# One minus the forget gate as a sigmoid of the negated logit, in a bidirectional gated recurrence

## The chip, the cores and the metric

The kernel runs on one core of one Trainium2 chip. The metric is the device time of one execution in microseconds (us); less is better. Engine names are those of the profile: PE (TensorE, matrix products), DVE (VectorE), ACT (ScalarE), POOL (GpSimd), SP (SyncE, which issues most transfers).

## The reference, cut to what matters

One encoder layer over 256 tokens of width 2048, in float32. Everything starts with a root mean square norm of `x` and one wide product with `w_in`, whose columns are nine groups of 2048. Five of them feed 16 heads of a gated linear recurrence that runs forward and backward; this is the part that the change touches:

```
def _hgrn2_direction(q, v, f_logit, lb, reverse):
    f = lb + (1.0 - lb) * jax.nn.sigmoid(f_logit)
    log_f = jnp.log(f)
    k = 1.0 - f
    ...
# chunks of 64 tokens, per head of 128
b = jnp.cumsum(log_f, axis=-2)
q_rel = q * jnp.exp(b - b_mid)
k_rel = k * jnp.exp(b_mid - b)
scores = q_rel @ k_rel^T, masked;   o = scores @ v + what the earlier chunks carry
```

`lb` is a lower bound per channel, a softmax over two learned rows. `o` of both directions is summed, normed per head and multiplied by `silu(z_a)`. The other four column groups are a gated convolution of width 3. Both branches go through `w_out`, are added to `x`, get a gated per-layer embedding (`p @ w_ple`, `w_ple_gate`) and a last norm.

## The kernel before, in words

PE does nearly all of its work on float32 operands that were split into a high and a low part of a faster matmul format. `Stream` brings blocks of weights by DMA into three buffers `raw`, and `split` (L120 to L122) makes the pair of parts: ACT copies with a cast (L121), DVE subtracts what the cast kept (L122). Five buffers `spl` hold the parts, and `get` runs three blocks ahead of PE. `gemm_in` makes one group of 256 channels from four such blocks of 1024 columns per partition; `evac` then brings its two banks out of PSUM (ACT's copy `r`, L487, then DVE's sum, L488).

The heads are handled in pairs (`i` = 0 to 7 in the helpers), and two pairs make a round of `two_pairs`, for i = 0, 2, 4, 6. In a round PE makes, for each of its two pairs, the forward logits, the backward logits and `q`. Then come the products for `v` and `z` of all four heads (`gemm_vz`). Work on the heads is laid over these products by a counter: `tick` counts PE's steps, `at(n, fn)` puts a function `n` steps later.

For one pair the steps are these, with 128 channels on the partitions and 256 tokens in a row:

- `mix_forgets` multiplies the logits `xf` (two directions, two heads, so 1024 columns) and `qt` by the norms (POOL, `by_norms`, L492). ACT makes the sigmoid of `xf` in place and of `qt` into `sg`; POOL makes `qt * sg`. Then, in four pieces of 256, ACT makes the logarithm of `f` into `lf` (L623) and DVE overwrites `xf` with `1 - f` (L627), as `sigmoid * noml + oml`, where `oml` is 1 - lb and `noml` its negative.
- `mix_pair` makes running sums `pf` and their distances `dd` on DVE, exponentials of them on ACT (L705 and L706, and a small one, `ge`, L703), then `kr` (`dd`) and `qr` (`pf`) as DVE products (L707, L708). POOL makes `kc`, `qc` and `kx` of them (L716, L722).
- `scores` are PE's products `scps` and `cx` (L735, L779); `outputs` are `o` (L797, L798), whose squares ACT sums up into `ss` (L802) and which DVE copies to `ogz` (L803).
- `last_two` of the round before runs inside the next one: `gate_two` makes `zt` times its sigmoid (ACT `sz`, L637, into the one buffer that `sg` uses too; POOL, L638), `finish_two` takes the root of `ss` (ACT, L642), its reciprocal (DVE, L643) and makes eight products `ogz` per round (DVE, L648), and `turn` transposes them on PE (`ogt`, L658).

The framework orders each engine's instructions by priority, except where a block is marked as fixed. Some calls raise the priority of what is needed soon (`high_priority`), the splits above all. Once built, each engine works off its list in order: an instruction that waits holds up all behind it on its engine.

Of the kernel before, what the change touches and what calls it, by code (L numbers as in the profile page):

```python
# [8 lines left out]
F32 = mybir.dt.float32  # L9
F32R = mybir.dt.float32r  # L10
U32 = mybir.dt.uint32
AF = mybir.ActivationFunctionType
ALU = mybir.AluOpType
# [4 lines left out]
P = 128  # L18
D = 2048
T = 256  # L20
# [117 lines left out]
def tile_hymba_encoder(  # L138
# [15 lines left out]
    act, dve, pool, pe = nc.scalar, nc.vector, nc.gpsimd, nc.tensor  # L154
    out2 = out[0].rearrange("(m p) d -> p m d", p=P)

    const = ctx.enter_context(tc.tile_pool(name="const", bufs=1))
# [7 lines left out]
    xp = xctx.enter_context(tc.tile_pool(name="xp", bufs=1, side="left"))  # L165
# [69 lines left out]
    rx, rb, rf, most, dummy = (few[:, 2 * j : 2 * j + 2] for j in range(5))  # L235
# [21 lines left out]
    cvw, th = vec[:, 3:6, :], vec[:, 6:10, :].rearrange("p (d j) c -> p d j c", d=2)  # L257


    wz = const.tile([P, P], F32, name="wz")  # L260
    dve.memset(wz, 0.0)

    act.activation(dummy[:, 0:1], wz[:, 0:1], AF.Copy)
# [6 lines left out]
    ident = const.tile([P, P], F32, name="ident")  # L270
# [1 line left out]
    ones = const.tile([P, 1], F32, name="ones")  # L272
    pool.memset(ones, 1.0)

    early = const.tile([P, 2048], F32, name="early")
    smask = early[:, 0:T]
    pool.memset(smask, 1.0)
    pool.memset(smask.rearrange("p (c t) -> p c t", t=CH)[:, :, 0:1], 0.0)
# [3 lines left out]
    for j in range(4):  # L282
        sgn = 1 if j < 2 else -1
        pool.affine_select(
            out=tri[:, j, :], in_=tri[:, j, :], compare_op=ALU.is_ge, fill=0.0, base=0,
# [9 lines left out]
        dve.memset(t, 0.0)  # L295


    mx = const.tile([P, 2, 16], F32, name="mx")
    et = const.tile([P, 2, 2, 16], F32, name="et")
    esum = const.tile([P, 2, 16], F32, name="esum")  # L300
    lb = const.tile([P, 2, 16], F32, name="lb")
    oml = const.tile([P, 2, 16], F32, name="oml")
    noml = const.tile([P, 2, 16], F32, name="noml")

    def lower_bounds():
        dve.tensor_tensor(out=mx, in0=th[:, :, 0, :], in1=th[:, :, 1, :], op=ALU.max)
        for j in range(2):
            dve.tensor_tensor(out=et[:, :, j, :], in0=th[:, :, j, :], in1=mx, op=ALU.subtract)
        act.activation(et, et, AF.Exp)
        dve.tensor_tensor(out=esum, in0=et[:, :, 0, :], in1=et[:, :, 1, :], op=ALU.add)  # L310
        dve.reciprocal(out=esum, in_=esum)
        dve.tensor_tensor(out=lb, in0=et[:, :, 0, :], in1=esum, op=ALU.mult)
        dve.tensor_scalar(lb, lb, 2.0**-63, None, op0=ALU.max)
        dve.tensor_tensor(out=oml, in0=et[:, :, 1, :], in1=esum, op=ALU.mult)
        dve.tensor_scalar(noml, oml, -1.0, None, op0=ALU.mult)


    pend = []
# [54 lines left out]
    rbc = const.tile([P, T], F32, name="rbc")  # L373
    rbc2 = early[:, T : 2 * T]
    ss8 = const.tile([P, 2, 4], F32, name="ss8")
    rw = [const.tile([P, P], F32, name=f"rw{m}") for m in range(2)]

    def load_tokens(m):
        nc.sync.dma_start(xf32[:, 8 * m : 8 * m + 8].rearrange("p k t -> p (k t)"), xtok[:, m])
# [12 lines left out]
    def x_norms():  # L392
        dve.tensor_reduce(out=rx, in_=ss8, op=ALU.add, axis=AX.X)
        act.activation(rx, rx, AF.Sqrt, bias=epst, scale=1.0 / D)
        dve.reciprocal(out=rx, in_=rx)
        for m in range(2):
            dve.tensor_copy(rw[m], rx[:, m : m + 1].broadcast_to([P, P]))

    def norms_spread():
        rps = psm.tile([P, 512], F32, tag="y", name="rps")  # L400
        for m in range(2):
            pe.matmul(rps[:, m * P : (m + 1) * P], lhsT=rw[m], rhs=ident, start=True, stop=True)
        dve.tensor_copy(rbc, rps[:, :T])  # L403
        dve.tensor_tensor(out=rbc2, in0=rbc, in1=rbc, op=ALU.mult)

# [84 lines left out]
    def by_norms(t, r, n):  # L490

        pool.tensor_tensor(out=t, in0=t, in1=r.unsqueeze(1).broadcast_to([P, n, T]), op=ALU.mult)  # L492
# [27 lines left out]
    ap_ = actx.enter_context(tc.tile_pool(name="ap", bufs=1, side="right"))  # L520
    for m in range(2):
        at(2 + m, lambda m=m: load_tokens(m))
    for c in range(4):
        at(6 + c, lambda c=c: x_squares(c))
    at(11, x_norms)
    at(14, norms_spread)


# [78 lines left out]
    def c64(t):  # L607
        return t.rearrange("p h (c t) -> p h c t", t=CH)

    def mix_forgets(i, xf, qt):  # L610

        by_norms(xf.rearrange("p a b t -> p (a b) t"), rbc, 4)
        by_norms(qt, rbc, 2)
        act.activation(xf, xf, AF.Sigmoid)
        sg = ap_.tile([P, 2, T], F32, tag="sg", name=f"sq{i}")
        act.activation(sg, qt, AF.Sigmoid)
        pool.tensor_tensor(out=qt, in0=qt, in1=sg, op=ALU.mult)

        lf = ap_.tile([P, 2, 2, T], F32, tag="lf", name=f"lf{i}")
        for d in range(2):  # L620
            for h in range(2):
                hd = 2 * i + h
                act.activation(  # L623
                    lf[:, d, h, :], xf[:, d, h, :], AF.Ln,
                    bias=lb[:, d, hd : hd + 1], scale=oml[:, d, hd : hd + 1],
                )
                dve.tensor_scalar(  # L627
                    xf[:, d, h, :], xf[:, d, h, :], noml[:, d, hd : hd + 1], oml[:, d, hd : hd + 1],
                    op0=ALU.mult, op1=ALU.add,
                )  # L630
        return lf

# [34 lines left out]
    def mix_pair(i, xf, qt, lf, here=False):  # L667
# [6 lines left out]
        dv = [dd[:, d] for d in range(2)]  # L674
        lfl = lf.rearrange("p a b c -> p (a b c)")
        for h in range(2):
            place(
                dve.tensor_tensor_scan(
                    out=pv[0][:, h, :], data0=smask, data1=lf[:, 0, h, :], initial=0.0, op0=ALU.mult, op1=ALU.add
# [5 lines left out]
                    out=pv[1][:, h, :], data0=lfl[:, o : o + T], data1=smask, initial=0.0, op0=ALU.add, op1=ALU.mult  # L685
# [4 lines left out]
        for h in range(2):  # L690
            dve.tensor_tensor(
                out=df4[:, h], in0=pf4[:, h], in1=pf4[:, h, :, 31:32].broadcast_to([P, 4, CH]), op=ALU.subtract
            )
            dve.tensor_tensor(
                out=db4[:, h], in0=pb4[:, h, :, 32:33].broadcast_to([P, 4, CH]), in1=pb4[:, h], op=ALU.subtract
# [8 lines left out]
        for d in range(2):  # L704
            act.activation(pv[d], dv[d], AF.Exp)  # L705
            act.activation(dv[d], dv[d], AF.Exp, scale=-1.0)  # L706
            dve.tensor_tensor(out=dv[d], in0=xf[:, d], in1=dv[d], op=ALU.mult)  # L707
            dve.tensor_tensor(out=pv[d], in0=qt, in1=pv[d], op=ALU.mult)  # L708
        qr, kr = pf, dd

# [3 lines left out]
        for dst, src, d, half in ((kc, kr, 0, 0), (qc, qr, 0, 1), (kc, kr, 1, 1), (qc, qr, 1, 0)):  # L714
            g = ge[:, d, :, 1 - half : 5 - half : 3]
            pool.tensor_tensor(  # L716
                out=c64(dst[:, d]), in0=c64(src[:, d, :, half * P : (half + 1) * P]),
                in1=g.unsqueeze(3).broadcast_to([P, 2, 2, CH]), op=ALU.mult,
# [93 lines left out]
    def two_pairs(i):  # L812
# [28 lines left out]
        for e in range(2):  # L841
            xf = ap_.tile([P, 2, 2, T], F32, tag="xf", name=f"xf{i + e}", bufs=2)
            qt = ap_.tile([P, 2, T], F32, tag="qt", name=f"qt{i + e}")
            first3 = i + e == 0

            kick = ({}, {}, {}) if i + e == 0 else (TURNED, {} if i and e else TURNED, TURNED)
            for j, (c, dst) in enumerate(((B_FF, xf[:, 0]), (B_FB, xf[:, 1]), (B_Q, qt))):

                acc, offset = acc3[j] if first3 else gemm_in(c, i + e, kick[j]), 500 if e and j == 2 else 200
                evac(acc, lambda m, dst=dst: dst[:, m, :], ap_, offset)  # L850

            def mix(e=e, xf=xf, qt=qt):
                forgets.append((xf, qt, mix_forgets(i + e, xf, qt)))
                if e == 0:
                    if before:
                        before()
                    steps.append(mix_pair(i, *forgets[0]))

            if first3:

                at(15, mix)
            else:
                mix()
# [5 lines left out]
        if i == 0:  # L869

            at(18, lambda: steps[0][0]())
            at(19, lambda: steps.append(mix_pair(i + 1, *forgets[1])))
            at(46, lambda: out(0))
            at(46, lambda: steps[1][0]())
            at(60, lambda: out(1))
            gemm_two(B_V, i, vt)
            xctx.close()
            xqp = xqctx.enter_context(tc.tile_pool(name="xqp", bufs=1, side="left", reuse_waits="tile"))
            xq.append(xqp.tile([P, len(VZ_SUMS), 4, 2, P], F32R, name="xsum"))
            xq.append(xqp.tile([P, 2, 512], F32, name="xd"))  # L880
            gemm_two(B_ZA, i, zt)
        else:

            at(4, lambda: steps[0][0]())
            gemm_vz(i, vt, zt)
            at(4, lambda: steps.append(mix_pair(i + 1, *forgets[1], here=True)))
            at(12, lambda: out(0))
            at(32, lambda: steps[1][0]())
            at(46, lambda: out(1))
# [34 lines left out]
    for i in range(8):  # L924
# [9 lines left out]
        for m in range(2):  # L934
            ct = 2 * i + m
            dve.tensor_scalar(cg[:, m, :], u[:, m, 0:T], cvw[:, 0, ct : ct + 1], None, op0=ALU.mult)
            for j in (1, 2):
                dve.scalar_tensor_tensor(
                    out=cg[:, m, :], in0=u[:, m, j : j + T], scalar=cvw[:, j, ct : ct + 1],
                    in1=cg[:, m, :], op0=ALU.mult, op1=ALU.add,  # L940
# [13 lines left out]
        for m in range(2):  # L954
            ct = 2 * i + m
            dve.scalar_tensor_tensor(
                out=hb[:, m, :], in0=hb[:, m, :], scalar=cnw[:, ct : ct + 1], in1=sz[:, m, :],
                op0=ALU.mult, op1=ALU.mult,
# [104 lines left out]
    for u in range(2):  # L1063
# [9 lines left out]
        for src, sums, main, other, scale in ((mixa, suma, psg, psm, False), (mixb, sumb, psm, psg, True)):  # L1073
            name = f"p{'ab'[scale]}{u}"
# [10 lines left out]
            for q1, q5, q6, q7 in half([acc[0:2], acc[2:4]], extra, ORDER, SUMS, parts, src, sums, False):  # L1085
                d, v, d7, v7 = tmps
# [179 lines left out]
```

## Time and profile before

| | us |
|---|---|
| median of 3 runs | 1111.57 |
| lowest and highest | 1110.87, 1111.96 |
| the profiled execution | 1112.2 |
| its span, first to last instruction | 1110.5 |

The granted clock of TensorE is 0.998 of the full one in the mean over the span. In the profile, busy time is given by engine; a group of instructions is named by line, engine, operation and tiles (out<-in), with its count, busy time, mean length and the idle time ahead of it with who ended that. A timeline row gives start and length in us from the span's start; "xN" at its end says that N like instructions were merged into it, and what stands in brackets is the idle time of the engine before it.

### The profile page before, as it was taken

Reading aid. Unit: us, or ns where it says so; the run is one execution under the profiler, and the core shown is the slowest. Engines: PE = TensorE matmul, PEld = TensorE weight load, DVE = VectorE, ACT = ScalarE, POOL = GpSimd, SP = SyncE. Lnnn points to the kernel's source line nnn. Section 1 sums busy time; section 2 is a strip of 40 time slices with the busy share of each in tenths; the row PEclk is TensorE's granted clock in tenths of the full one; section 3 lists DMA queues with packets and bytes.
Section 4 is the critical chain, followed back from the end, with each engine's and each line's share of the span. In section 5 each row is a group of like instructions: output and inputs, shape, how many; then the busy total and the mean of one; then the engine's idle time right before and its main releaser. Section 6 shows DMA issues by size and latency. Waiting matters only on the chain.

```text
span 1110.5 us, 16882 instructions
## 1 busy us (share of the span) xinstructions
PE 1100.5 (99%) x6455; PEld 945.7 (85%) x6455; DVE 851.4 (77%) x1127; ACT 677.3 (61%) x946; POOL 269.1 (24%) x215
## 2 busy tenths in 40 slices
PE   9999999999999999999999999999999999999997
PEld 8888888888888888888888888888888888888886
DVE  7799578896889778997657758856667888887673
ACT  6786577667876697575545535535546575575562
POOL 1045015203530325043334223424331000000101
PEclk9999999999999999999999999999999999999999
DMA  9755454564457744758999998999979887887542
GB/s 340 272 187 190 153 190 157 171 242 153 161 162 258 292 152 152 231 172 228 298 310 250 270 334 231 282 345 254 288 196 306 318 299 286 286 312 253 193 133 76
DMA packets 69808, 260.44 MB, mean 235 GB/s; under 512 B 7008, under 2 KB 16608, under 8 KB 52192
## 3 DMA queue, kind: packets, MB, share of 16 engines
q1 hardware_dynamic: 60480, 242.25, 62.1%
q0 software_dynamic: 8960, 16.78, 10.0%
q8 instruction: 51, 0.84, 0.3%
q10 hardware_dynamic: 288, 0.34, 0.1%
q14 instruction: 29, 0.24, 0.1%
HBM read 257.25 MB, written 35.65 MB: 264 GB/s over the span
## 4 chain that ended last, share of the span: by engine, by line
PE 98%; DMA 1%; ACT 0%; SPq 0%; DVE 0%; DVEq 0%; issue 0%; ACTq 0%
PE a L427 37%; PE a L425 19%; PE avz L547 3%; PE avz L548 3%; PE avz L549 3%; PE pg L1027 3%; PE pg L1026 3%; PE pg L1028 3%; PE pa L547 2%; PE pa L548 2%; PE pa L549 2%; PE a L446 1%; PE a L448 1%; PE a L447 1%; PE pb_sc L548 1%; PE pb_sc L549 1%
## 5 line engine op out<-in xcount | busy, mean ns | idle before, releaser
L122 DVE TENSOR_TENSOR spl<-raw,spl 128x1024 fp32r<-128x1024 f32 (+2 forms) x419 | 505.0, 1219 | 163.6 <-ACT spl L121 160.2
L427 PE MATMUL a<-xs,spl 128*128 128x512 f32 x1792 | 617.3, 395 | 0.6 <-ACT spl L121 0.6
L121 ACT CAST spl<-raw 128x1024 fp32r<-128x1024 f32 (+2 forms) x419 | 414.1, 999 | 255.0 <-PE a L425 81.9
L425 PE MATMUL a<-xs,spl 128*128 128x256 f32 x1792 | 483.8, 278 | 0.0
L427 PEld LDWEIGHTS a<-xs,spl 128*128 128x128 f32 x1792 | 332.2, 188 | 73.6 <-ACT spl L121 1.0
L425 PEld LDWEIGHTS a<-xs,spl 128*128 128x128 f32 x1792 | 334.6, 188 | 5.8 <-DVE spl L122 0.5
L1143 POOL TENSOR_TENSOR hh<-hh,fw 128x512 f32<-128x512 f32 (+1 forms) x9 | 11.0, 1227 | 250.7 <-ACT gt L1142 248.0
L487 ACT COPY r<-a 128x256 f32<-128x256 f32 x112 | 40.5, 368 | 37.3 <-PE a L425 35.8
L547 PE MATMUL avz<-spl,xs 128*128 128x512 f32 x138 | 54.0, 391 | 0.0
L549 PE MATMUL avz<-spl,xs 128*128 128x512 f32 x138 | 53.7, 389 | 0.0
L548 PE MATMUL avz<-spl,xs 128*128 128x512 f32 x138 | 53.7, 389 | 0.0
L1026 PE MATMUL pg<-spl,ht 128*128 128x512 f32 (+1 forms) x120 | 45.2, 377 | 0.0
L1027 PE MATMUL pg<-spl,ht 128*128 128x512 f32 (+1 forms) x120 | 45.1, 376 | 0.0
L1028 PE MATMUL pg<-spl,ht 128*128 128x512 f32 (+1 forms) x120 | 45.0, 375 | 0.0
L716 POOL TENSOR_TENSOR qc<-pf,ge 128x256 f32<-128x256 f32 x16 | 18.3, 1148 | 105.8 <-ACT dd L706 91.8
L492 POOL TENSOR_TENSOR xf<-xf,rbc 128x1024 f32<-128x1024 f32 x8 | 19.9, 2486 | 94.0 <-DVE rbc L403 50.2
L121 ACT CAST spl<-early 128x1024 fp32r<-128x1024 f32 (+1 forms) x29 | 28.7, 990 | 19.1 <-PE pb_y L549 7.5
L122 DVE TENSOR_TENSOR spl<-early,spl 128x1024 fp32r<-128x1024 f32 (+1 forms) x29 | 32.9, 1147 | 9.2 <-ACT spl L121 8.8
L547 PE MATMUL pa<-spl,mixa 128*128 128x512 f32 x88 | 34.5, 392 | 0.0
L549 PE MATMUL pa<-spl,mixa 128*128 128x512 f32 x88 | 34.3, 389 | 0.0
L548 PE MATMUL pa<-spl,mixa 128*128 128x512 f32 x88 | 34.2, 389 | 0.0
L716 POOL TENSOR_TENSOR kc<-dd,ge 128x256 f32<-128x256 f32 x16 | 27.7, 1728 | 19.8 <-DVE dd L707 13.6
(321 smaller groups left out, 1641.7 us busy)
## 6 DMA issues: line engine op xcount, KB each, us to landing
raw<-in_w_in_dram SPq DMA_DIRECT2D x106, 1024.0 KB, 6.9
raw<-in_w_in_dram SPq DMA_DIRECT2D x100, 256.0 KB, 3.9
raw<-in_w_out_dram SPq DMA_DIRECT2D x36, 512.0 KB, 5.2
sums<-in_w_out_dram SPq DMA_DIRECT2D x32, 512.0 KB, 10.6
raw<-in_w_in_dram SPq DMA_DIRECT2D x26, 512.0 KB, 5.2
raw<-sums SPq DMA_DIRECT2D x13, 1024.0 KB, 5.3
raw<-in_w_gate_dram SPq DMA_DIRECT2D x9, 1024.0 KB, 5.1
sums<-in_w_out_dram POOLq DMA_DIRECT2D x16, 512.0 KB, 10.1
```

Source lines behind the costliest of these rows:

```text
L121: self.nc.scalar.copy(out=v[:, :, 0], in_=r)
L122: self.nc.vector.tensor_tensor(out=v[:, :, 1], in0=r, in1=v[:, :, 0], op=ALU.subtract)
L425: pe.matmul(a[:, :T], lhsT=lhsT, rhs=xs[:, kt, 0, :], start=False, stop=(kt == NKT - 1))
L427: pe.matmul(a, lhsT=lhsT, rhs=xs[:, kt, :, :].rearrange("p s n -> p (s n)"), start=(kt == 0), stop=False)
L487: act.copy(out=r, in_=acc[m][:, 1, :])
L547: pe.matmul(acc, lhsT=ah, rhs=w[:, 0], start=start, stop=False)
L548: pe.matmul(acc, lhsT=ah, rhs=w[:, 1], start=False, stop=False)
L549: pe.matmul(acc, lhsT=al, rhs=w[:, 0], start=False, stop=stop)
L716: pool.tensor_tensor(out=c64(dst[:, d]), in0=c64(src[:, d, :, half * P : (half + 1) * P]), in1=g.unsqueeze(3).broadcast_to([P, 2, 2, CH]), ...
L1026: pe.matmul(acc[m], lhsT=lh, rhs=wh, start=(kt == 0), stop=False)
L1027: pe.matmul(acc[m], lhsT=lh, rhs=wl, start=False, stop=False)
L1028: pe.matmul(acc[m], lhsT=ll, rhs=wh, start=False, stop=(kt == nk - 1))
```

## The change

`1 - f` is (1 - lb) times (1 - sigmoid), and that is (1 - lb) times the sigmoid of the negated logit. So:

- `mix_forgets` makes the sigmoid of the logits into `lf` and a second one, with scale -1, in place in `xf`. The logarithm then works in place on `lf`. The four DVE operations that made `1 - f` are gone, and so is `noml`.
- In `mix_pair` the product that makes `kr` takes the factor in: four scalar_tensor_tensor of 128x256 (`xf * oml * dd`) stand for two tensor_tensor of 128x512.
- The zeros of PE's warm-up lie in the part of `early` that later holds the first score mask; three small tiles of `lower_bounds` go to another pool, and the spread norms `rw` use a buffer of the tile `s`.

```
-    wz = const.tile([P, P], F32, name="wz")
+    early = const.tile([P, 2048], F32, name="early")
+    wz = early[:, 1024 : 1024 + P]
     dve.memset(wz, 0.0)
...
-    mx = const.tile([P, 2, 16], F32, name="mx")
-    et = const.tile([P, 2, 2, 16], F32, name="et")
-    esum = const.tile([P, 2, 16], F32, name="esum")
+    mx = xp.tile([P, 2, 16], F32, name="mx")
+    et = xp.tile([P, 2, 2, 16], F32, name="et")
+    esum = xp.tile([P, 2, 16], F32, name="esum")
...
-    noml = const.tile([P, 2, 16], F32, name="noml")
...
-        dve.tensor_scalar(noml, oml, -1.0, None, op0=ALU.mult)
...
-    rw = [const.tile([P, P], F32, name=f"rw{m}") for m in range(2)]
...
+        rw.append(ap_.tile([P, 2, P], F32, tag="s", name="rw"))
...
-        act.activation(xf, xf, AF.Sigmoid)
+        lf = ap_.tile([P, 2, 2, T], F32, tag="lf", name=f"lf{i}")
+        act.activation(lf, xf, AF.Sigmoid)
         sg = ap_.tile([P, 2, T], F32, tag="sg", name=f"sq{i}")
         act.activation(sg, qt, AF.Sigmoid)
+        act.activation(xf, xf, AF.Sigmoid, scale=-1.0)
         pool.tensor_tensor(out=qt, in0=qt, in1=sg, op=ALU.mult)
 
-        lf = ap_.tile([P, 2, 2, T], F32, tag="lf", name=f"lf{i}")
         for d in range(2):
             for h in range(2):
                 hd = 2 * i + h
                 act.activation(
-                    lf[:, d, h, :], xf[:, d, h, :], AF.Ln,
+                    lf[:, d, h, :], lf[:, d, h, :], AF.Ln,
                     bias=lb[:, d, hd : hd + 1], scale=oml[:, d, hd : hd + 1],
                 )
-                dve.tensor_scalar(
-                    xf[:, d, h, :], xf[:, d, h, :], noml[:, d, hd : hd + 1], oml[:, d, hd : hd + 1],
-                    op0=ALU.mult, op1=ALU.add,
-                )
...
             act.activation(dv[d], dv[d], AF.Exp, scale=-1.0)
-            dve.tensor_tensor(out=dv[d], in0=xf[:, d], in1=dv[d], op=ALU.mult)
+            for h in range(2):
+                dve.scalar_tensor_tensor(
+                    out=dv[d][:, h], in0=xf[:, d, h], scalar=oml[:, d, 2 * i + h : 2 * i + h + 1], in1=dv[d][:, h],
+                    op0=ALU.mult, op1=ALU.mult,
+                )
             dve.tensor_tensor(out=pv[d], in0=qt, in1=pv[d], op=ALU.mult)
```

With other instructions the framework's order comes out otherwise. PE's order is the same but for names. The lists of ACT, DVE and POOL differ in the rounds; the place below is in the round i = 4, and it repeats at i = 6. There PE makes the logits of pair 5, while ACT, DVE and POOL work on pair 4 and finish pairs 2 and 3 (`zt`, `ss`, `ogz`). A number behind a name is the buffer's.

DVE before, from the reciprocal of `ss` to behind the last product `ogz`:

```order
L643 RECIPROCAL ss_1332<-ss_1332 128x8
L122 TENSOR_TENSOR spl_2830<-raw_2809,spl_2830 128x4x256
L708 TENSOR_TENSOR pf_2755<-qt_2354,pf_2755 128x512
L122 TENSOR_TENSOR spl_2851<-raw_2849,spl_2851 128x4x256
L648 SCALAR_TENSOR_TENSOR ogz_2447<-ogz_2447,ss_1332,zt_1331 128x128 x2
L648 SCALAR_TENSOR_TENSOR ogz_2704<-ogz_2704,ss_1332,zt_1331 128x128 x2
L122 TENSOR_TENSOR spl_2878<-raw_2849,spl_2878 128x4x256
L648 SCALAR_TENSOR_TENSOR ogz_2447<-ogz_2447,ss_1332,zt_1331 128x128 x2
L122 TENSOR_TENSOR spl_2899<-raw_2897,spl_2899 128x4x256
L488 TENSOR_TENSOR xf_2786<-a_5_0_2788,r 128x256
L488 TENSOR_TENSOR xf_2786<-a_5_1_2789,r 128x256
L648 SCALAR_TENSOR_TENSOR ogz_2704<-ogz_2704,ss_1332,zt_1331 128x128 x2
```

DVE in the changed kernel, from the second product with `qt` to behind the last `ogz`:

```order
L709 TENSOR_TENSOR pf_2744<-qt_2344,pf_2744 128x512
L705 SCALAR_TENSOR_TENSOR dd_2745<-xf_2343,oml,dd_2745 128x256 x2
L122 TENSOR_TENSOR spl_2869<-raw_2840,spl_2869 128x4x256
L122 TENSOR_TENSOR spl_2890<-raw_2888,spl_2890 128x4x256
L488 TENSOR_TENSOR xf_2777<-a_5_0_2779,r 128x256
L488 TENSOR_TENSOR xf_2777<-a_5_1_2780,r 128x256
L640 RECIPROCAL ss_1326<-ss_1326 128x8
L645 SCALAR_TENSOR_TENSOR ogz_2439<-ogz_2439,ss_1326,zt_1325 128x128 x3
L122 TENSOR_TENSOR spl_2919<-raw_2888,spl_2919 128x4x256
L645 SCALAR_TENSOR_TENSOR ogz_2439<-ogz_2439,ss_1326,zt_1325 128x128
L122 TENSOR_TENSOR spl_2940<-raw_2938,spl_2940 128x4x256
L645 SCALAR_TENSOR_TENSOR ogz_2696<-ogz_2696,ss_1326,zt_1325 128x128 x4
```

The reciprocal has moved behind the two sums into `xf`, and all eight `ogz` behind it; two more splits stand between them.

ACT before, from the first exponential of pair 4 to the first `sz`:

```order
L705 ACT_TABLE_LOAD
L705 ACTIVATE pf_2755<-dd_2756 128x512
L642 ACT_TABLE_LOAD
L642 ACTIVATE ss_1332<-ss_1332,epst 128x8
L121 CAST spl_2830<-raw_2809 128x4x256
L616 ACT_TABLE_LOAD
L616 ACTIVATE sq_2737<-qt_2354 128x512
L121 CAST spl_2851<-raw_2849 128x4x256
L637 ACTIVATE sz_0_2749<-zt_1331 128x512
```

ACT in the changed kernel, from the first `sz` to the root:

```order
L634 ACTIVATE sz_0_2738<-zt_1325 128x512
L703 ACT_TABLE_LOAD
L703 ACTIVATE dd_2745<-dd_2745 128x512
L121 CAST spl_2869<-raw_2840 128x4x256
L634 ACT_TABLE_LOAD
L634 ACTIVATE sz_1_2741<-zt_1325 128x512
L121 CAST spl_2890<-raw_2888 128x4x256
L487 COPY r<-a_5_0_2779 128x256
L487 COPY r<-a_5_1_2780 128x256
L639 ACT_TABLE_LOAD
L639 ACTIVATE ss_1326<-ss_1326,epst 128x8
```

The root of `ss` stood ahead of the first `sz` and now stands behind both and the two copies `r`; the exponentials of pair 4 have moved ahead of it.

POOL before, from the second multiplication of `qt`:

```order
L617 TENSOR_TENSOR qt_2354<-qt_2354,sq_2737 128x512
L638 TENSOR_TENSOR zt_1331<-zt_1331,sz_0_2749 128x512
L716 TENSOR_TENSOR qc_2779<-pf_2755,ge_2765 128x256
L638 TENSOR_TENSOR zt_1331<-zt_1331,sz_1_2752 128x512
L716 TENSOR_TENSOR kc_2778<-dd_2756,ge_2765 128x256
L716 TENSOR_TENSOR qc_2779<-pf_2755,ge_2765 128x256
```

POOL in the changed kernel, from the same place:

```order
L619 TENSOR_TENSOR qt_2344<-qt_2344,sq_2730 128x512
L717 TENSOR_TENSOR qc_2770<-pf_2744,ge_2754 128x256
L635 TENSOR_TENSOR zt_1325<-zt_1325,sz_0_2738 128x512
L717 TENSOR_TENSOR qc_2770<-pf_2744,ge_2754 128x256
L717 TENSOR_TENSOR kc_2769<-dd_2745,ge_2754 128x256
L723 TENSOR_TENSOR kx_2775<-kc_2769,ge_2754 128x512
L635 TENSOR_TENSOR zt_1325<-zt_1325,sz_1_2741 128x512
```

The second `zt` now has `qc`, `kc` and `kx` between it and the first.

More of the change, by code (lines that the diff above doesn't have):

```diff
@@ L273, in tile_hymba_encoder @@
     pool.memset(ones, 1.0)
-    early = const.tile([P, 2048], F32, name="early")
     smask = early[:, 0:T]
@@ L395, in x_norms @@
         dve.reciprocal(out=rx, in_=rx)
+        rw.append(ap_.tile([P, 2, P], F32, tag="s", name="rw"))
         for m in range(2):
-            dve.tensor_copy(rw[m], rx[:, m : m + 1].broadcast_to([P, P]))
+            dve.tensor_copy(rw[0][:, m], rx[:, m : m + 1].broadcast_to([P, P]))
+    rw = []
     def norms_spread():
@@ L401, in norms_spread @@
         for m in range(2):
-            pe.matmul(rps[:, m * P : (m + 1) * P], lhsT=rw[m], rhs=ident, start=True, stop=True)
+            pe.matmul(rps[:, m * P : (m + 1) * P], lhsT=rw[0][:, m], rhs=ident, start=True, stop=True)
         dve.tensor_copy(rbc, rps[:, :T])
```

## The prediction

> **What bounds the kernel now.** First the page's busy times and its chain, then TensorE's own waits.
>
> ```profile
> PE 1100.5 (99%) x6455; PEld 945.7 (85%) x6455; DVE 851.4 (77%) x1127; ACT 677.3 (61%) x946; POOL 269.1 (24%) x215
> PE 98%; DMA 1%; ACT 0%; SPq 0%; DVE 0%; DVEq 0%; issue 0%; ACTq 0%
> PE wps L266 <- DVE wz L261: 1.1, 1, 1.1
> PE a L427 <- ACT spl L121: 0.6, 1, 0.6
> ```
>
> The last two lines are all the waits of TensorE (PE): 1.7 us, both at the start. From there to its last matmul it always has the next operand. So an operation taken from another engine gains nothing by itself, and the question is only whether some operand of PE comes late in the new order. Gains are bounded by that 1.7 us.
>
> The reserve of the weight stream is in the idle time of ScalarE (ACT), from the page's groups, and by shape:
>
> ```profile
> L121 ACT CAST spl<-raw 128x1024 fp32r<-128x1024 f32 (+2 forms) x419 | 414.1, 999 | 255.0 <-PE a L425 81.9
> L614 ACT ACTIVATE xf<-xf 128x1024 f32<-128x1024 f32 x8 | 8.5, 1062 | 6.9 <-POOL xf L492 6.9
> L627 DVE TENSOR_SCALAR xf<-xf,noml,oml 128x256 f32<-128x256 f32 x32 | 14.8, 472 | 4.6 <-ACT lf L623 4.6
> L707 DVE TENSOR_TENSOR dd<-xf,dd 128x512 f32<-128x512 f32 x16 | 13.6, 851 | 0.6 <-ACT dd L706 0.6
> L938 DVE SCALAR_TENSOR_TENSOR cg<-ub,vec,cg 128x256 f32<-128x256 f32 x32 | 14.5, 477 | 0.2
> ```
>
> The casts that feed PE stood idle 255.0 us, 81.9 of it because PE had not yet freed a buffer: they run ahead of PE.
>
> **The change part by part, by sums.** ACT gains eight 128x1024 sigmoids: 8 x 1.06 = 8.5 us. The new order has 48 table loads for 52, 4 x 1.28 = 5.1 us less, so ACT nets +3.4 us. VectorE (DVE) loses 32 tensor_scalars (14.8 us) and 16 products (13.6), and gets 32 fused products of 128x256, which before shows at L938: 32 x 0.477 = 15.3. DVE nets -13.1 us. All of this lies beside PE and is worth 0, covered by the idle time above; without that cover ACT's sigmoids would cost up to 8.5.
>
> The small edits: the warm-up's zeros are still DVE's first memset; POOL's memset of the score masks now waits for the warm-up matmuls, but POOL has nothing due for 50 us, as this row shows:
>
> ```profile
> 54.29 2.40 POOL L492 TENSOR_TENSOR xf<-xf,rbc 128x1024 f32<-128x1024 f32 x1 [50.18 <-DVE rbc L403]
> ```
>
> `noml`, `mx`, `et`, `esum` and `rw` are 0 too, between +0.2 and -0.2 us (an estimate, one small DVE operation either way).
>
> **The place where the order matters.** The scheduler placed things anew. PE's stream is the same, so what counts is each operand's date against PE's. In the pairs i = 4 and i = 6, the transposes of the gated heads (`ogt`, L658) now depend on work that was pushed back. Before, timeline rows of PE, then DVE, then ACT (start, length):
>
> ```profile
> 300.01 0.39 PE L427 MATMUL a<-xs,spl 128*128 128x512 f32 x1
> 300.36 1.03 PE L658 MATMUL ogt<-ident,ogz 128*128 128x128 f32 x8
> 301.15 0.48 PE L427 MATMUL a<-xs,spl 128*128 128x512 f32 x1
> 417.78 1.03 PE L658 MATMUL ogt<-ident,ogz 128*128 128x128 f32 x8
> 284.04 0.19 DVE L643 RECIPROCAL ss<-ss 128x8 f32<-128x8 f32 x1
> 290.84 1.48 DVE L648 SCALAR_TENSOR_TENSOR ogz<-ogz,ss,zt 128x128 f32<-128x128 f32 x4 [1.20 <-POOL zt L638]
> 292.25 1.21 DVE L122 TENSOR_TENSOR spl<-raw,spl 128x1024 fp32r<-128x1024 f32 x1
> 297.00 0.61 DVE L648 SCALAR_TENSOR_TENSOR ogz<-ogz,ss,zt 128x128 f32<-128x128 f32 x2
> 414.43 0.61 DVE L648 SCALAR_TENSOR_TENSOR ogz<-ogz,ss,zt 128x128 f32<-128x128 f32 x2
> 276.94 0.28 ACT L802 ACTIVATE jk<-o 128x128 f32<-128x128 f32 x1 [0.90 <-PE o L798]
> 279.88 1.28 ACT L705 ACT_TABLE_LOAD   x1
> 281.28 0.64 ACT L705 ACTIVATE pf<-dd 128x512 f32<-128x512 f32 x1
> 281.94 1.28 ACT L642 ACT_TABLE_LOAD   x1
> 283.23 0.30 ACT L642 ACTIVATE ss<-ss,epst 128x8 f32<-128x8 f32 x1
> 293.71 0.64 ACT L487 COPY r<-a 128x256 f32<-128x256 f32 x2
> ```
>
> Eight `ogz` products end at 297.61, PE wants the first four at 300.36 and the others after four transposes of 0.1 us, at 300.76: a reserve of 3 us. At i = 6 it is 415.04 against 417.78.
>
> In the new order ACT's square root `ss` stands behind both COPYs of `r`. The added sigmoid ahead (its start-to-start cost is about 0.97 us) is swallowed by the 0.90 idle at 276.94, so the table load of 279.88 stays within 0.1. From there to the end of the COPYs, 294.35 before, ACT loses one table load and `ss` (1.28 + 0.2) and gains three 128x512 exponentials that came later before (3 x 0.52): 294.4. Then a table load 1.28, the root 0.30, the reciprocal 0.2: 296.2. Behind it on DVE stand 3 `ogz` (0.9), a split (1.13), 1 `ogz` (0.3), a split (1.13), 4 `ogz` (1.1), together 4.5: 300.7. That would just meet 300.76. This is the low end: no loss.
>
> But the same stretch has the GpSimd (POOL) products that these `ogz` need, and they and DVE hold each other up:
>
> ```profile
> 286.49 1.29 POOL L617 TENSOR_TENSOR qt<-qt,sq 128x512 f32<-128x512 f32 x1 [2.40 <-ACT sq L616]
> 288.53 2.28 POOL L638 TENSOR_TENSOR zt<-zt,sz 128x512 f32<-128x512 f32 x1 [0.74 <-ACT sz L637]
> 290.77 0.62 POOL L716 TENSOR_TENSOR qc<-pf,ge 128x256 f32<-128x256 f32 x1
> 292.94 1.68 POOL L638 TENSOR_TENSOR zt<-zt,sz 128x512 f32<-128x512 f32 x1 [1.56 <-ACT sz L637]
> 298.28 5.01 POOL L716 TENSOR_TENSOR kc<-dd,ge 128x256 f32<-128x256 f32 x1 [3.66 <-DVE dd L707]
> 305.51 1.05 POOL L722 TENSOR_TENSOR kx<-kc,ge 128x512 f32<-128x512 f32 x1
> 288.43 1.22 DVE L122 TENSOR_TENSOR spl<-raw,spl 128x1024 fp32r<-128x1024 f32 x1
> 298.12 1.22 DVE L122 TENSOR_TENSOR spl<-raw,spl 128x1024 fp32r<-128x1024 f32 x1
> 299.26 0.68 DVE L708 TENSOR_TENSOR pf<-qt,pf 128x512 f32<-128x512 f32 x1
> 299.86 1.22 DVE L122 TENSOR_TENSOR spl<-raw,spl 128x1024 fp32r<-128x1024 f32 x1
> 301.60 1.22 DVE L122 TENSOR_TENSOR spl<-raw,spl 128x1024 fp32r<-128x1024 f32 x1
> 302.73 0.42 DVE L488 TENSOR_TENSOR xf<-a,r 128x256 f32<-128x256 f32 x1
> ```
>
> Starts on DVE are 1.14 apart behind a split and 0.60 behind `pf` (298.12, 299.26, 299.86). POOL's `kc`, of the shape for which `qc` took 0.62, took 5.01 while DVE went through split, `pf`, split, `dd` and split, and ended 0.57 after DVE turned to an operation that reads PSUM (302.73). Likewise the first `zt` took 2.28 and the second 1.68, each under a split (288.43 to 289.65, and the one of 292.25 that ended at 293.46) and each ending 1.16 to 1.17 after it. So DVE products from SBUF and POOL products run one after the other.
>
> Before, only `qc` stood between the two `zt`. Now `qc`, `kc` and `kx` do, and DVE's `pf` and fused `dd`, which came behind the `ogz` before, fall into the same window. It opens when POOL's `qt` ends, 287.8. From there to the end of the second `zt`, POOL has qc 0.6, zt 1.16, qc 0.6, kc 0.6, kx 1.05, zt 1.16 = 5.2; DVE has pf 0.6, split 1.13, pf 0.6, two fused dd 0.8, two splits 2.26 = 5.4. One after the other: 287.8 + 10.6 = 298.4. The `ogz` that read `zt` queue behind, and the splits behind them: 298.4 + 4.5 = 302.9, which is 2.1 us past 300.76. Nothing else on PE can go first, since its queue is in order. I take this value, because the rows show the two engines excluding each other in just this stretch. Two such places: +4.2 us.
>
> The Trainium skill, SBUF — State Buffer, section "Who interferes with whom", says that a DVE instruction with two SBUF inputs contends with a GpSimd instruction that reads SBUF, and that whichever issues first keeps the pair for that whole instruction. By that, `kc` should have waited for one split; here it waited through four DVE instructions, so waiting can cost more than the page says. By its rule alone, turn and turn about, the sum is the same 4.2.
>
> Two other dates move little. At i = 2 the order has the root where it was. Pair 7 is the nearest:
>
> ```profile
> 495.94 1.92 POOL L722 TENSOR_TENSOR kx<-kc,ge 128x512 f32<-128x512 f32 x1
> 499.07 1.16 PE L779 MATMUL cx<-qc,kx 128*128 128x128 f32 x8
> ```
>
> `kx` is ready 1.2 us early; two fused products for one (2 x 0.477 for 0.851, +0.1) at two steps ahead of it, and POOL's waits for them, eat part of that: I take 0, at most 0.6. The split made at 292.25 is the operand of the last quarter of the product that ends at 300.36. A pair of matmuls takes 0.35 (300.01 to 300.36) and a split serves eight, 2.8 us: it is used from 297.6, four us later. The splits' delay of 2 to 3 us stays inside that: 0.
>
> **The sum.** The profiled execution took 1112.2 us (span 1110.5), 0.6 over the median 1111.57. 1112.2 + 2 x 2.1 = 1116.4 there, so 1115.8 against the median.
>
> **The rivals.**
> 1. No change: DVE and POOL fit into each other's gaps, and `ogz` ends by 300.8 as the plain sum of ACT and DVE says. It decides by one number: if the eighth `ogz` ends before the fifth transpose is due, the loss is 0. For it: DVE waits for ACT in this stretch, so POOL finds gaps. Against: the 5.01 above. Time 1111.6; up to 1.1 us a place still counts here (2.2 in all). Chance 0.30.
> 2. POOL starves for several DVE instructions on end, as `kc` did. DVE's first forced pause is then behind the split that follows the fused products: 287.8 + 0.6 + 1.14 + 0.6 + 0.8 + 1.14, and about 0.6 for an exponential of ACT that `dd` waits for, is 292.7. Only there do qc (0.6) and the first `zt` (1.16) run, to 294.5. The second `sz` of ACT shares its one buffer with the first, so it waits for that `zt`: sz 0.6, cast 1.0, COPYs 0.6, table 1.28, root 0.3 end at 298.3. With the reciprocal and the rest of the second `zt`, 299.1; plus 4.5 is 303.6, or 2.9 a place: 1117.4. Chance 0.18.
> 3. The sigmoid makes the casts late everywhere: 8 x 0.97 = 7.8, 1119.4. Against it the 81.9 us of ACT waiting for PE. Chance 0.03.
> 4. Faster, since DVE has 13 us less: only the 0.6 at the start could shrink. Chance 0.02.
>
> The main case, 1.1 to 2.6 a place, has 0.47.
>
> **How the numbers follow.** A measurement of this kernel tells from no change about 0.2%, 2.2 us. Slower: 0.47 + 0.18 + 0.03 = 0.68; within: 0.30; faster: 0.02. Range: down to 1111.2 (all of rival 1 but its lowest tail), up to 1118.2 (rival 2 plus 0.6 at pair 7). The likeliest case alone gives 1113.8 to 1116.8.
>
> **What would show it.** PE waits of about 2 us at the transposes, put down to DVE `ogz`, near 300 and near 420, and nowhere else; the reciprocal of `ss` at 296 to 298; `zt` behind `kx`. Right in mechanism but wrong in size if the waits are there and short. Wrong altogether if PE shows no waits beyond 1.7 us, or shows them on casts.

## The result, and the profile after

| | before | changed |
|---|---|---|
| median, us | 1111.65 | 1117.55 |
| lowest and highest | 1110.87, 1112.02 | 1116.63, 1120.32 |
| runs | 6 | 6 |
| the profiled execution | 1112.2 | 1117.67 |
| its span | 1110.5 | 1116.0 |

The ratio is 1.0057, 95% interval 1.0045 to 1.0070: the change makes the kernel 0.6% slower. (Here and below a ratio is taken over all runs on one chip; it is not the quotient of the two medians.) The forecast was 1115.8 us with a range of 1111.2 to 1118.2. Sign and range hold, but most of the loss is not where the prediction put it.

First the page of the changed kernel: the busy times, and the chain by engine.

```profile
PE 1105.7 (99%) x6455; PEld 946.0 (85%) x6455; DVE 842.8 (76%) x1110; ACT 678.5 (61%) x950; POOL 261.9 (23%) x215
PE 90%; ACT 3%; DVE 2%; POOL 2%; issue 1%; DMA 1%; DVEq 0%; SPq 0%; POOLq 0%; ACTq 0%
```

DVE lost 8.6 us of work (851.4 before) and ACT gained 1.2 (677.3). The number that matters is PE's: the same 6455 matmuls kept it busy 1105.7 us instead of 1100.5. A wait would show as idle time; here PE is *busy* 5.2 us longer. So the list of PE's waits cannot hold the answer, though the waits that were forecast are in it:

```profile
PE wps L267 <- DVE early L262: 1.1, 1, 1.1
PE ogt L655 <- DVE ogz L645: 0.4, 2, 0.2
```

PE's timeline at the two places, start and length, in the changed kernel:

```profile
299.63 0.80 PE L655 MATMUL ogt<-ident,ogz 128*128 128x128 f32 x5
300.63 0.59 PE L655 MATMUL ogt<-ident,ogz 128*128 128x128 f32 x3 [0.20 <-DVE ogz L645]
300.99 0.47 PE L427 MATMUL a<-xs,spl 128*128 128x512 f32 x1
...
417.66 0.80 PE L655 MATMUL ogt<-ident,ogz 128*128 128x128 f32 x5
418.66 0.59 PE L655 MATMUL ogt<-ident,ogz 128*128 128x128 f32 x3 [0.20 <-DVE ogz L645]
419.02 0.47 PE L427 MATMUL a<-xs,spl 128*128 128x512 f32 x1
```

From the first transpose to the next product PE took 1.36 us at each place (299.63 to 300.99, 417.66 to 419.02), where before took 0.79 (300.36 to 301.15, and 417.78 to 418.57). That is 0.57 us a place, 1.1 in all. The 0.20 in brackets is less than that: the fifth transpose starts at 300.10 and its record lasts 0.33, so the bracket counts only from 300.43 to 300.63, while in the kernel before one transpose starts 0.11 behind the other. The sixth transpose starts 0.06 after the seventh `ogz` has ended (300.57), and that is the piece it reads: `finish_two` makes the four pieces of a pair token half by token half, `turn` reads them head by head.

The rest is found by pairing PE's matmuls by their number in the stream, since both kernels run the same ones in the same order. The 5,244th and the 6,003rd are these, before and then after:

```profile
840.75 0.39 PE L549 MATMUL pa<-spl,mixa 128*128 128x512 f32 x1
1010.03 0.39 PE L1028 MATMUL pg<-spl,ht 128*128 128x512 f32 x1
```

```profile
841.29 0.40 PE L549 MATMUL pa<-spl,mixa 128*128 128x512 f32 x1
1015.08 0.40 PE L1029 MATMUL pg<-spl,ht 128*128 128x512 f32 x1
```

The changed kernel is 0.54 us behind at the first and 5.05 at the second: 4.5 us are lost over 759 matmuls, practically all of it in the 715 of them that belong to the output projection (`half`, moving operand `spl`, stationary operand `mixa`, `mixb`, `suma` or `sumb`). The change does not touch an instruction there. Two windows of that stage, with PE's busy time, count of matmuls, granted clock, DMA share and GB/s, before and then after:

```profile
840.00:920.00 80.00, 80.00 (x355) 1.00 0.92 313
920.00:1000.00 80.00, 80.00 (x363) 1.00 0.82 289
```

```profile
840.00:920.00 80.00, 79.93 (x344) 1.00 0.89 301
920.00:1000.00 80.00, 80.00 (x355) 1.00 0.81 282
```

PE is full in all four and the clock is 1.00 in all four, but 699 matmuls fit where 718 did. In the groups by line and shape, cut to this stage (count, busy us, mean ns of one), before and then after:

```profile
L547 PE MATMUL pb_sc<-spl,mixb 128*128 128x512 f32 x48 | 18.7, 389 | 0.0
L548 PE MATMUL pb_sc<-spl,mixb 128*128 128x512 f32 x48 | 18.7, 389 | 0.0
L549 PE MATMUL pb_sc<-spl,mixb 128*128 128x512 f32 x48 | 18.7, 389 | 0.0
```

```profile
L548 PE MATMUL pb_sc<-spl,mixb 128*128 128x512 f32 x48 | 19.0, 396 | 0.0
L547 PE MATMUL pb_sc<-spl,mixb 128*128 128x512 f32 x48 | 18.9, 394 | 0.0
L549 PE MATMUL pb_sc<-spl,mixb 128*128 128x512 f32 x48 | 18.9, 393 | 0.0
```

Every group of the stage went from 389 to 391 ns before to between 392 and 399, without a wait. 4.5 us over 715 is 6.3 ns a matmul, about what the means show. The record of a matmul overlaps the next one: from start to start the matmuls of this stage are 227 ns apart in the mean before and 233 after, and the expectations below go by this distance.

What did change for these matmuls is where their operands lie. `noml` (128 bytes on each partition) is gone, and `wz`, `mx`, `et`, `esum` and `rw` (2048 bytes together) went into other tiles. All large tiles that are laid out from the left of SBUF (`raw`, `spl`, `xs`, `hh`, `ht`, `sumb`) start 2176 bytes lower; `mixa`, `mixb` and `suma`, laid out from the right, stay. In the built kernels `spl` begins at byte 54208 before and 52032 after, `mixb` at 147392 in both: modulo 1024 that is 960 and 960 before, 832 and 960 after; modulo 256 it is 192 and 192, then 64 and 192.

### The profile page after: what moved, and what is told of

It is laid out like the page before. It is cut to its first block, busy times and chain, and to the rows that moved or that the text cites. A ratio compares the mean times of both kernels' runs of the same rounds, so it can differ in the third digit from the quotient of the medians.

```text
span 1116.0 us, 16883 instructions
## 1 busy us (share of the span) xinstructions
PE 1105.7 (99%) x6455; PEld 946.0 (85%) x6455; DVE 842.8 (76%) x1110; ACT 678.5 (61%) x950; POOL 261.9 (23%) x215
## 4 chain that ended last, share of the span: by engine, by line
PE 90%; ACT 3%; DVE 2%; POOL 2%; issue 1%; DMA 1%; DVEq 0%; SPq 0%; POOLq 0%; ACTq 0%
PE a L427 33%; PE a L425 17%; PE avz L547 3%; PE avz L549 3%; PE avz L548 3%; PE pg L1027 3%; PE pg L1029 3%; PE pg L1028 3%; PE pa L548 1%; PE pa L549 1%; PE pa L547 1%; PE a L448 1%; PE a L446 1%; PE a L447 1%; PE pb_sc L548 1%; PE pb_sc L547 1%
## 5 line engine op out<-in xcount | busy, mean ns | idle before, releaser
L122 DVE TENSOR_TENSOR spl<-raw,spl 128x1024 fp32r<-128x1024 f32 (+2 forms) x419 | 497.6, 1203 | 181.6 <-ACT spl L121 179.9
L944 POOL TENSOR_TENSOR cg<-cg,hb 128x512 f32<-128x512 f32 x8 | 14.6, 1822 | 78.0 <-DVE hb L488 78.0
```

Source lines behind the costliest of these rows:

```text
L122: self.nc.vector.tensor_tensor(out=v[:, :, 1], in0=r, in1=v[:, :, 0], op=ALU.subtract)
```

## The experiments

Two theories. **Placement**: a matmul is slower when its moving and its stationary operand do not agree in their byte offset. **Order**: all of the loss comes from the new order of ACT, DVE and POOL. An unused tile among the constants moves the left side without moving work. The first four ran on one chip, on which the kernel before took 1112.64 us (median of 23), the next four on another (1113.00, median of 23), the last two on a third.

### The shift alone, in the kernel before

```
     oml = const.tile([P, 2, 16], F32, name="oml")
+    gap = const.tile([P, 32], F32, name="gap")
+    pool.memset(gap, 0.0)
     noml = const.tile([P, 2, 16], F32, name="noml")
```

> The kernel before, with one unused 128-byte tile (and one memset of it on GpSimd) among the constants: `raw`, `spl`, `xs`, `hh`, `ht` and `sumb` lie 128 bytes higher, `mixa`, `mixb` and `suma` stay, and no other instruction differs. Placement theory (the output projection's matmuls take longer when `spl` and the `mix` tiles do not lie at the same offset): 1116 us, 1115 to 1117, with the 512-wide matmuls after 840 us about 232 to 236 ns apart where the kernel before has 227, and no wait at `ogt`. Order theory (all of the change's loss comes from the new order of ACT, DVE and POOL): 1111.6 us, like before, 227 ns throughout.

Measured: 1118.22 us, ratio 1.0041 (1.0026 to 1.0056). PE's waits and the same three groups:

```profile
PE wps L266 <- DVE wz L261: 1.1, 1, 1.1
PE a L429 <- ACT spl L121: 0.3, 1, 0.3
```

```profile
L549 PE MATMUL pb_sc<-spl,mixb 128*128 128x512 f32 x48 | 19.0, 395 | 0.0
L550 PE MATMUL pb_sc<-spl,mixb 128*128 128x512 f32 x48 | 18.9, 395 | 0.0
L551 PE MATMUL pb_sc<-spl,mixb 128*128 128x512 f32 x48 | 18.9, 394 | 0.0
```

No wait at `ogt`, the old math and the old order, and yet 394 to 395 ns and most of the loss. The order theory falls for this part: 128 bytes of nothing cost 0.4%. The median lies above the 1115 to 1117 expected, and not only because this chip's kernel before is 1 us slower. In the profiled execution, the fastest of the six at 1115.51, the output projection took 3.9 us longer than in the kernel before; where the slower runs lost more is not shown.

### The shift undone, in the changed kernel

The same two lines behind `oml` in the changed kernel, so that the left side stands 2048 instead of 2176 bytes lower (960 of 1024 again).

> The changed kernel with one unused 128-byte tile (and a memset) among the constants, so that `spl` and the tiles beside it lie 2048 instead of 2176 bytes lower than before. Placement theory: the 512-wide matmuls after 840 us go back to 227 ns; what is left is the two waits at `ogt`, about 0.5 us each: 1112.7 us, 1112.2 to 1113.2. Order theory: 1117.5 us, as the changed kernel.

Measured: 1114.54 us, ratio 1.0018 (1.0007 to 1.0028).

```profile
L549 PE MATMUL pb_sc<-spl,mixb 128*128 128x512 f32 x48 | 18.7, 389 | 0.0
L550 PE MATMUL pb_sc<-spl,mixb 128*128 128x512 f32 x48 | 18.7, 389 | 0.0
L551 PE MATMUL pb_sc<-spl,mixb 128*128 128x512 f32 x48 | 18.7, 389 | 0.0
```

The stage is back at 389 ns. The 1112.7 expected were reckoned from a kernel before at 1111.6; on this chip that was 1112.64, so what is left is 1.9 us, where two waits of 0.5 to 0.6 were expected.

### The sigmoid and the product alone, without and with a tile in `noml`'s place

The two lines of math and the dropped `noml`, with the five small tiles where before has them (left side 128 bytes lower); then the same with the 128 bytes of `gap` put back (nothing moved).

> The sigmoid of the negated logit, the product with `oml` and the dropped tile `noml` alone; `wz`, `mx`, `et`, `esum` and `rw` stay where before has them. `spl` lies 128 bytes lower than before, by the dropped `noml`. Placement theory: 1117.3 us, 1116.5 to 1118, 229 to 241 ns between the 512-wide matmuls after 840 us. If instead the moved small tiles were what costs: 1112.7 us. Order theory: 1117.5 us.

> As the run with the sigmoid and the product alone, with an unused 128-byte tile where `noml` was, so that every large tile lies where it lies in the kernel before. Placement theory: 1112.7 us, 1112.2 to 1113.2, 227 ns after 840 us, two waits at `ogt` of about 0.5 us. Order theory: 1117.5 us.

Measured: 1117.82 us, ratio 1.0050 (1.0031 to 1.0069), without the tile, and 1114.52 us, 1.0012 (1.0003 to 1.0022), with it. One group of the first and of the second:

```profile
L545 PE MATMUL pb_sc<-spl,mixb 128*128 128x512 f32 x48 | 19.0, 395 | 0.0
```

```profile
L547 PE MATMUL pb_sc<-spl,mixb 128*128 128x512 f32 x48 | 18.7, 389 | 0.0
```

The two kernels with the tile (1114.52 and 1114.54) differ by all the moved small tiles, and do not differ in time. So no cost of the moves can be told at intervals of 1 us to either side, the math and its order cost 1 to 2 us, and the 128 bytes of `noml` the rest. The 1112.7 expected with the tile was missed here as in the run before. Set against the kernel before matmul by matmul, both profiled executions lost 1.2 us at the two places of `ogt`; what else they lost lies at different places, 1.9 us between 674 and 752 in this one, 1.3 near 757 and 767 (behind waits for split weights) and 1.1 in the output projection (with another such wait) in the other.

### The other operand moved instead

```
-    mixa = mixp.tile([P, NH * 2 * T + 8], F32R, name="mixa")[:, : NH * 2 * T]
+    mixa = mixp.tile([P, NH * 2 * T + 40], F32R, name="mixa")[:, : NH * 2 * T]
```

> The changed kernel with the pad behind `mixa` at 40 instead of 8 floats: `mixa`, `mixb` and `suma` lie 128 bytes lower and stand again at the offset of `spl` (832 of 1024, for both), which itself stays where the changed kernel has it. If the relative offset of the matmul's two operands decides: 389 ns mean of one in the output projection and the time of the run with the 128-byte tile (about 1114 us on this chip). If it is the place of `spl` alone: 394 to 398 ns and 1117.5 us, as the changed kernel. Order theory: 1117.5 us too.

Measured: 1114.96 us, ratio 1.0015 (1.0004 to 1.0025), with `spl` where the changed kernel has it.

```profile
L547 PE MATMUL pb_sc<-spl,mixb 128*128 128x512 f32 x48 | 18.7, 389 | 0.0
```

So it is the one operand against the other that counts, not where either lies by itself. In the kernel before it is the pad of 8 floats behind `mixa` that puts both at 192 modulo 256; what it is worth was not tried.

### The transposes one step later

```
-                    at(32, lambda e=e: turn(i + e, ogs[e], "yx"[e]))
+                    at(33, lambda e=e: turn(i + e, ogs[e], "yx"[e]))
```

This on top of the changed kernel with the 128-byte tile.

> The changed kernel with the 128-byte tile, and the transposes `ogt` queued one step of the schedule later (33 instead of 32), so that `ogz` is long written when PE comes to them. If the two waits at `ogt` are all that is left of the change's loss: no wait at `ogt`, 0.8 to 1.2 us under the run with the tile alone, and within 0.1% of the kernel before. If the late `ogz` only shows a delay that PE meets elsewhere: the time of the run with the tile alone, with a wait of the same size at another place.

Measured: 1112.99 us, ratio 0.9999 (0.9988 to 1.0009).

```profile
PE wps L267 <- DVE early L262: 1.1, 1, 1.1
PE pa L550 <- DVE spl L122: 0.6, 1, 0.6
```

The wait at `ogt` is gone and with it the rest of the loss: 1.97 us under the run with the moved `mixa`, which shared its chip and has the same order but for this step. That is more than the 1.14 which the two places show. Matmul by matmul, the two profiled executions end 2.35 us apart: 1.1 comes at the two places and 1.5 between 674 and 752, where the run with the moved `mixa` is in the slower rhythm described last below and this one is not (0.3 the other way comes in the output projection). Whether the medians differ for the same reason is not shown. Both causes removed, the kernel stands level with the one before. It isn't faster: PE was full before, and DVE's 8.6 us had nobody waiting for them.

### Which offsets cost

The unused tile at 640, 1152, 384 and 192 bytes, so that `spl` stands 512, 1024, 256 and 64 bytes above the place at which it agrees with the `mix` tiles; one execution each.

> The changed kernel with an unused tile of 640 bytes: `spl` lies 512 bytes above the place at which it agrees with the `mix` tiles modulo 1024. If the offset counts modulo 512 or less: 389 ns mean in the output projection. If it counts modulo 1024 or more: 394 ns or above. Order theory: no difference to the changed kernel's 394 to 398 ns.

> The changed kernel with an unused tile of 1152 bytes: `spl` lies 1024 bytes above the place of the run with the 128-byte tile, at the same offset modulo 1024. Placement theory: 389 ns mean in the output projection, as there. If the offset counts modulo 2048: 394 ns or above.

> The changed kernel with an unused tile of 384 bytes: `spl` lies 256 bytes above the place at which it agrees with the `mix` tiles. If an offset of a multiple of 512 bytes is what keeps the matmuls apart: 394 ns or above in the output projection. If a multiple of 256 does: 389 ns, as with 512 and 1024.

> The changed kernel with an unused tile of 192 bytes: `spl` lies 64 bytes above the place at which it agrees with the `mix` tiles. If only multiples of 256 or 512 are free of the loss: 394 ns or above in the output projection, some 5 us in all. If 64 suffices and 128 is a case of its own: 389 ns.

The groups at 256 bytes, then at 64:

```profile
L549 PE MATMUL pb_sc<-spl,mixb 128*128 128x512 f32 x48 | 18.7, 389 | 0.0
L550 PE MATMUL pb_sc<-spl,mixb 128*128 128x512 f32 x48 | 18.7, 389 | 0.0
L551 PE MATMUL pb_sc<-spl,mixb 128*128 128x512 f32 x48 | 18.7, 389 | 0.0
```

```profile
L549 PE MATMUL pb_sc<-spl,mixb 128*128 128x512 f32 x48 | 18.9, 393 | 0.0
L550 PE MATMUL pb_sc<-spl,mixb 128*128 128x512 f32 x48 | 18.8, 392 | 0.0
L551 PE MATMUL pb_sc<-spl,mixb 128*128 128x512 f32 x48 | 18.7, 390 | 0.0
```

| `spl` against `mixb`, bytes | mean ns of the three `pb_sc` groups | run |
|---|---|---|
| 0 | 389, 389, 389 | before; the changed kernel with the tile, or with `mixa` moved |
| +64 | 393, 392, 390 | tile of 192 bytes |
| +128 | 395, 395, 394 | the shift alone, in the kernel before |
| -128 | 396, 394, 393 | the changed kernel |
| +256, +512, +1024 | 389, 389, 389 | tiles of 384, 640, 1152 bytes |

Of the offsets tried, the multiples of 256 bytes are free, 128 costs most and 64 about half. At 64 bytes less was lost than the 394 ns expected, and of the two readings put to the 256-byte run the multiple of 256 stands. The four single times (1115.76, 1115.16, 1117.86 and 1118.27 us, the last two on a chip where one run of the kernel before took 1114.27) can't be told apart by this: the run at 256 bytes has 2.7 us of waits for split operands at other places, the one at 64 bytes 2.3.

## Why the prediction was right or wrong

**PE bounds the kernel, and work taken from other engines gains nothing.** Right. DVE fell by 8.6 us rather than the 13.1 reckoned, and ACT rose by 1.2 rather than 3.4; the largest miss is the fused products, 32 of 0.737 us where 0.477 was taken from L938. There every one took between 0.466 and 0.487, here they go from 0.472 to 1.529; that POOL's products beside them make the difference is likely, but was not tried apart. None of PE's waits is put down to them. Their group in the changed kernel:

```profile
L705 DVE SCALAR_TENSOR_TENSOR dd<-xf,oml,dd 128x256 f32<-128x256 f32 x32 | 22.3, 737 | 2.0 <-ACT dd L703 1.9
```

**The place.** Right: PE waits at the transposes of `ogz` near 300 and 418 and at no other place in the rounds, put down to DVE.

**Its size.** Wrong: 2 x 2.1 us was forecast, 2 x 0.57 came. The rows of the changed kernel, POOL and then DVE:

```profile
285.31 1.29 POOL L619 TENSOR_TENSOR qt<-qt,sq 128x512 f32<-128x512 f32 x1
287.46 1.47 POOL L717 TENSOR_TENSOR qc<-pf,ge 128x256 f32<-128x256 f32 x1 [0.87 <-DVE pf L709]
288.90 1.76 POOL L635 TENSOR_TENSOR zt<-zt,sz 128x512 f32<-128x512 f32 x1
290.61 0.80 POOL L717 TENSOR_TENSOR qc<-pf,ge 128x256 f32<-128x256 f32 x1
291.84 1.47 POOL L717 TENSOR_TENSOR kc<-dd,ge 128x256 f32<-128x256 f32 x1 [0.42 <-DVE dd L705]
293.39 1.91 POOL L723 TENSOR_TENSOR kx<-kc,ge 128x512 f32<-128x512 f32 x1
295.26 1.30 POOL L635 TENSOR_TENSOR zt<-zt,sz 128x512 f32<-128x512 f32 x1
...
289.41 2.29 DVE L705 SCALAR_TENSOR_TENSOR dd<-xf,oml,dd 128x256 f32<-128x256 f32 x2
291.62 1.21 DVE L122 TENSOR_TENSOR spl<-raw,spl 128x1024 fp32r<-128x1024 f32 x1
295.22 0.20 DVE L640 RECIPROCAL ss<-ss 128x8 f32<-128x8 f32 x1 [0.16 <-ACT ss L639]
299.70 1.13 DVE L645 SCALAR_TENSOR_TENSOR ogz<-ogz,ss,zt 128x128 f32<-128x128 f32 x4
```

The prediction let the window open when `qt` ends, at 287.8, and gave POOL and DVE 10.6 us one after the other, to 298.4, then 4.5 us to the last `ogz`. Measured: `qt` ends at 286.60, the second `zt` at 296.56, which is 10.0 us later, and the last `ogz` at 300.83, 4.3 after that. So `zt` stood behind `kx` as said, and the serial sum was right within 0.6; but the loss is a small difference of large dates, and four misses of the same sign took most of it. The start was taken from a row of before, and it came 1.2 us earlier; 0.7 of that is that PE was ahead here (299.63 against 300.36 at the first transpose; the 0.6 us wait at the start of before is not in this execution), so PE wanted the fifth piece at 300.03, not at 300.76, and only 0.5 counts. The serial stretch was 0.6 too long and the tail 0.2. The last 0.2 is a slip of the prediction: it held the end of the eighth `ogz` against the date of the fifth transpose, though the pieces come one by one and the eighth is wanted three transposes later. The reciprocal came at 295.22, just ahead of the 296 to 298 named. By the prediction's own bounds 0.57 a place lies in the "up to 1.1" counted with its first rival and not in the 1.1 to 2.6 of its main case: the place and the cause of these waits were right, their price was not. Its sign of being wrong altogether, no waits beyond 1.7 us, could not decide: the waits in the list come to 1.5 us, since the 0.6 at the start is gone and a bracket holds 0.20 of each 0.57.

**The rivals.** "`ogz` in time" is refuted by the waits and by its own number (the eighth `ogz` ended at 300.83, the fifth transpose was due at 300.03), though its 300.7 for the last `ogz` was nearest and its band holds the loss that came. "POOL starves" is refuted for this place by `kc` and `qc` at 1.47 us, where `kc` had 5.01 before. The Trainium skill, SBUF — State Buffer, section "Who interferes with whom", has the holder keep the shared ports for one instruction; the new rows fit that (one split runs when `kc` starts at 291.84, and `kc` ends 0.5 us after it). The rows of before do not: `kc` took 5.01 at both places (298.28 and 415.72), 3.87 at 182.00 and 3.35 at 99.71. Late casts and a gain did not come.

**The small edits, "0, between +0.2 and -0.2".** This is the term that failed most: 4.5 us stood where it had put 0, because it priced instructions, and the cost of dropping `noml` is not in one. The run with only the 128 bytes (ratio 1.0041) and the two with them put back (1.0018, 1.0012) show it. In the profiled execution the account is: 0.7 us gained ahead of 299.63, 1.1 lost at `ogt`, 4.5 in the output projection, and small change: 5.06 at PE's last matmul, 5.5 in the span. The median stood 1.75 us above the forecast because a cause of 4.5 us was missing and another was taken 3 us too large. That the forecast came out near the measurement is luck: without the 4.5 us, the waits that were foreseen, 1.1 us, would not have stood clear of the 2.2 us that the prediction itself took for no change.

## What to carry to other kernels

When a tile is dropped or moved, look at where the tiles behind it now start, above all the two operands of a matmul that come from different ends of SBUF: here they had to agree modulo 256 bytes, and an unused tile or a pad of a few floats was the remedy. When a change in an unrelated stage appears as more busy time at the same count and the same clock, compare the mean length of one instruction by shape before looking for waits. And take the dates of a forecast against PE's own progress, not from the clock of the old trace.

## What was not expected of the hardware

**A matmul's rate depends on the offset of its operands.** The record of a 128x512 matmul took 389 ns in the mean with operands at the same offset modulo 256 bytes and up to 399 when they differed by 128, in a stream with no wait and a granted clock of 1.00; over the output projection that is 4.5 us. The Trainium skill, SBUF — State Buffer, section "Who interferes with whom", gives TensorE independent ports for the moving operand and for the weights; the runs with 128 unused bytes and with `mixa` moved disagree as far as the rate goes, for there only the offset of one against the other counts. That the two reads of SBUF collide is the obvious reading but was only argued. One observation says more about which reads: the groups `epb<-spl,sumb`, whose operands agree in every kernel, also went to 392 to 394 ns in the changed one. In the run with the shift alone, the 56 of these matmuls that stand ahead of another with `sumb` stayed at 390 ns, and the 16 that stand ahead of one with a `mix` tile took 397. So a matmul is slowed by the place of the next one's stationary operand as well as by that of its own.

**PE can fall into a slower rhythm.** Between 680 and 740 us (products `a`, whose two operands agree in their offset in every kernel) the profiled executions fall into two groups. The kernel before, and then the math alone with the tile, same clock, nobody waiting:

```profile
680.00:740.00 60.00, 60.00 (x347) 1.00 0.98 291
```

```profile
680.00:740.00 60.00, 60.00 (x342) 1.00 0.96 290
```

Five of the twelve executions profiled made 341 or 342 matmuls there, the others 347 to 349: about 1 us. In all five, set against before matmul by matmul, it follows matmuls between 674 and 680 us that start 0.04 to 1.4 us late, and goes on at an even 2% to about 752 us, 1.3 us in all. A late start alone does not set it: the runs at 64 and at 1024 bytes have one of 0.17 us at the same matmuls and keep the rate. All five have the new math and order, but so have five of the seven others, among them the changed kernel itself; the two executions without them do not show it, which is too few to say that the kernel before is free of it. It may be a part of why runs of one kernel on the later chips spread over 4 us (1111.18 to 1115.36 for the kernel before), but no profile of such a slower run of the kernel before was taken. What sets the rhythm was not tried.
